# Attention with each score computed once, queries on partitions and weights turned by TensorE, in a one-core transformer layer

## The chip, the core and the metric

The kernel runs on one core of a Trainium2 chip. Its metric is the device time of one execution in microseconds (us): the median of three runs is 1499.16 us (1499.1 to 1499.41). The engines in the profile are TensorE (PE, with its weight loads as PEld), VectorE (DVE), ScalarE (ACT), GpSimd (POOL) and the sync engine (SP), which issues DMAs.

## The reference

One layer over 1024 positions of width 1024, all in float32. Two attentions run side by side, each with 8 heads of width 64, and a gated merge and a feed-forward block follow:

```python
h = rms_norm(x, norm1); proj = h @ w_in            # q,k,v of both attentions, forget logits, gates
# forgetting attention, causal:  c = cumsum(log_sigmoid(f))
sc = q @ k.T / 8 + c[query] - c[key];  p = softmax(where(key <= query, sc, -1e30));  o_a = p @ v
# band attention: own chunk of 64 and the 8 chunks before, plus a bias by clipped distance
sc = where(valid, q @ k.T / 8 + rel_bias[clip(query - key)], -1e30);  o_b = softmax(sc) @ v
merged = sigmoid(g_a) * (o_a @ w_branch_a) + sigmoid(g_b) * (o_b @ w_branch_b)
x = x + merged @ w_out
x = x + relu(rms_norm(x, norm2) @ w_up)**2 @ w_down;   return rms_norm(x, final_norm)
```

## The kernel before

Every product is made of matmuls on operands that are split in a high part (rounded to fp32r) and a low part (the rest). ACT makes the high part (L282 `split`, L167 for weights), DVE or POOL the low part (L283, L169), and TensorE adds high·high, high·low and low·high (`product`, L220). The stages follow one another: norm and first gates, the projections of q, k, v and the gates by Strassen units of 7 products (`strassen_steps`), attention, the branch products (`branch`, tiles `m`), the output product (`o`), the up projection and the down projection. q and k lie in DRAM for each head as `qk_dram` (128 rows: high parts twice against high and low) and `sk_dram` (64 rows: the remaining low part), v as `v_dram` (high and low halves).

Attention has 16 heads of 1024 queries, cut in 8 blocks of 128: first the 8 band heads (pairs `pr` 0 to 3, each query block sees up to 5 key blocks), then the 8 forgetting heads (`pr` 4 to 7, up to 8 key blocks). Each head takes two steps:

- `shifts` (two heads ahead of its use): scores with queries on partitions (L505, high parts only; L508 adds the causal mask by a matmul), a DVE instruction that adds the bias and takes the least value of a row (L512, sign turned, so this is the row's maximum), and a transpose of these 8 columns to a row in DRAM (L517, `m_rows`). It is needed for a safe softmax only.
- `attend`: scores again, now with keys on partitions (tiles `st`: L739 with `qk`, L747 with `sk`, whose extra rows carry masks and the row's shift; L755 adds the causal mask or the distance bias by more matmuls), ACT's exp (L759), a split of the weights `p` in `th` (ACT, L282) and `tl` (DVE, L283), and three matmuls into the output bank `pv` (L762, L763, L764). Columns of ones beside v give the row sums. ACT copies the bank out (L771, L774, L775), and `normalise` sends the row sums through DRAM, takes the reciprocal and multiplies (L793).

TensorE's and the other engines' order within attention is that of a scheduler, except where a call goes through `Ordered` (`TO`, `VO`, `AO`, `LO`), which keeps the program's order on that engine (its instructions all have one line, L96). `psg`, `pss`, `pst` and `psv` are PSUM pools of 1, 3, 3 and 1 banks. 16 fillers (`filler`, 12 matmuls each), the branch products of the heads that are done, run beside the forgetting heads. While the last two gate units (6 and 7) run, `shifts` of the first two heads are spread between their products by the table `AHEAD`. After the last head come the branch products of the forgetting heads (192 matmuls, L220 `m`, results joined by POOL at L846). Exp and sigmoid are different tables of ACT. The sigmoid of the gates is at L396, with the gates' stores to `z_dram`.

Of the kernel before, what the change touches and what calls it, by code (L numbers as in the profile page):

```python
# [18 lines left out]
P = 128  # L19
# [15 lines left out]
EARLY, AHEAD = 3, (0, 0, 0, 3, 4, 3, 3, 3)  # L35
LO_POOL = lambda n: False

BC, PB = 2, 5

SK = HD + 18  # L40

NORM = (2, 6, 10, 14)
BIAS = 1
GPOOL = ()
# [11 lines left out]
FILL = lambda n: 16 if n <= 18 else 16 - (n - 18) * 16 // 14  # L56

# [12 lines left out]
def pieces(width):  # L70
    if width <= 512:
        return [(0, max(width, 256), width)]
    if width - 512 >= 256:
        return [(0, 512, 512), (512, width - 512, width - 512)]
    return [(0, width - 256, width - 256), (width - 256, 256, 256)]
# [7 lines left out]
def hybrid_block(ctx: ExitStack, tc: tile.TileContext, xT, xN, g1, wall, wf, fb, relb, relt, rows, g2, g3, outT):  # L83
# [14 lines left out]
    VO, TO, AO, LO = Ordered(V), Ordered(T), Ordered(A), Ordered(nc.sync)  # L98
# [20 lines left out]
    identr = cpool.tile([P, P], F32R, tag="identr", name="identr")  # L119
    V.tensor_copy(identr, ident)  # L120

    masks = []
    for n, (step, cm) in enumerate(((-1, 1), (1, -1))):
        m = cpool.tile([P, 3, P], F32R, tag=f"mask{n}", name=f"mask{n}")
        raw = tmp("raw")[:, 0:3 * P].rearrange("p (n q) -> p n q", q=P)
        G.memset(raw, 0.0)
        G.affine_select(out=raw[:, 1, :], in_=raw[:, 1, :], compare_op=ALU.is_ge, fill=BIG, base=0,
                        pattern=[[step, P]], channel_multiplier=cm)
        G.tensor_copy(m, raw)
        masks.append(m)  # L130
# [8 lines left out]
    ncq = cpool.tile([P, 8, NH], F32, tag="ncq", name="ncq")  # L139
# [7 lines left out]
    m_rows = dram("m_rows", [16, 2, S])  # L147
    o_dram = dram("o_dram", [4, P, S])
    d_dram = dram("d_dram", [8, 2, S])
# [243 lines left out]
    def gate_out(ps, c, h, eng=V):  # L393
        t = etile("zt")
        eng.tensor_tensor(t, ps, rstd[:, hs(h)], op=ALU.mult)
        A.activation(t, t, AF.Sigmoid)  # L396
        store(z_dram[c, :, hs(h)], t)

# [49 lines left out]
    def forget_columns():  # L448
        pt = pst.tile([P, 8, NH], F32, tag="st", name="cqt")
        for h in range(2):  # L450
            c = tp.tile([NH, HALF], F32, tag="t", name="cr", bufs=8)
            load(c, c_dram[:, hs(h)])
            for i in range(4):
                T.transpose(pt[:, 4 * h + i, :], c[:, i * P:(i + 1) * P], ident[0:NH, 0:NH])
        V.tensor_scalar(ncq, pt, -1.0, None, op0=ALU.mult)

    heads = [(pr, hh) for pr in range(8) for hh in range(2)]

    def load_bias(pr, hh):

        fox = pr >= 4
        head = 2 * (pr % 4) + hh
        bc = aps.tile([P, S], F32, tag="bc", name=f"bc{pr}_{hh}", bufs=BC)
        if fox:
            load(bc, c_dram[head:head + 1, :].to_broadcast([P, S]))
            return bc, None, lambda: None
        load(bc[:, :BAND], relb[head])
        near = tmp("near")[:, 0:256]  # L470
        load(near, relt[head])
        far = aps.tile([P, 1], F32, tag="far", name="far", bufs=2)
        nb = [aps.tile([P, 256], F32R, tag="nb" + x, name=f"nb{x}{pr}_{hh}", bufs=3) for x in "hl"]

        def finish():
            tc.keep_in_program_order(V.tensor_copy(far, bc[:, 0:1]))
            for t in (bc[:, :BAND], near):
                A.activation(t, t, AF.Identity, scale=-1.0, bias=far)
            G.memset(bc[0:64, BAND - 64:BAND], BIG)
            G.memset(bc[64:128, 0:64], BIG)  # L480
            split(nb, near, G)

        return bc, nb, finish

    def load_head(pr, hh):
        qk = apq[(2 * pr + hh) % 3].tile([P, 2, S], F32R, tag="qk", name=f"qk{pr}_{hh}")
        loads.append(load_r(qk, qk_dram[2 * pr + hh]).ins)
        return qk

    loads = []  # L490

    def shifts(pr, hh, qk, bc, ps_s, ps_t):

        fox = pr >= 4
        mn = aps.tile([P, 8], F32, tag="mn", name=f"mn{pr}_{hh}", bufs=2)
        for i in range(8):
            j0 = 0 if fox else max(0, i - 4)
            W = (i + 1 - j0) * P
            st = aps.tile([P, 4], F32, tag="st", name="st", bufs=4)
            prev, x = 3.0e38, 0  # L500
            for s0, n, v in pieces(W):
                ks = j0 * P + s0
                ps = ps_s.tile([P, HALF], F32, tag="d", name="s")
                diag = fox and s0 + v == W
                T.matmul(ps[:, :n], qk[:, 1, i * P:(i + 1) * P], qk[:, 0, ks:ks + n], start=True, stop=not diag)  # L505
                if diag:
                    d = v - 256 if v > P else 0
                    T.matmul(ps[:, d:d + 256], identr, masks[0][:, 0:2, :] if v > P else masks[0][:, 1:3, :],  # L508
                             start=False, stop=True)
                b0 = s0 if fox else (4 - i + j0) * P + s0  # L510
                out = mn[:, i:i + 1] if s0 + v == W else st[:, x:x + 1]
                V.tensor_tensor_reduce(ps[:, :v], ps[:, :v], bc[:, b0:b0 + v], 1.0, prev, ALU.add, ALU.min, out)  # L512
                prev, x = out, x + 1
            if i < 7:
                yield
        pt = ps_t.tile([P, HALF], F32, tag="d", name="mt")
        T.transpose(pt[0:8, 0:P], mn, ident)  # L517
        mr = aps.tile([8, 2, P], F32R, tag="mr", name=f"mr{pr}_{hh}", bufs=2)
        split((mr[:, 0, :], mr[:, 1, :]), pt[0:8, 0:P], V)
        store(m_rows[2 * pr + hh].rearrange("r (i k) -> i r k", k=P), mr.bitcast(F32))  # L520
        yield
# [118 lines left out]
    tiles = [load_bias(*hd) for hd in heads[:2]]  # L640
    for t in tiles:
        t[2]()
# [10 lines left out]
    apq = [pool(astack, f"apq{n}", "right") for n in range(2)][::-1]  # L653
    for n in range(2):
        tiles[n] = (load_head(*heads[n]), *tiles[n])
    ahead = chain(*[shifts(*heads[n], *tiles[n][:2], psd[1], psd[1]) for n in range(2)])

    for n, ins in enumerate(chain(steps, last)):
        with tc.issue_after(ins):
            for _ in range(AHEAD[n]):  # L660
                next(ahead, None)
# [10 lines left out]
    ap_, apv, apq2, ap0 = [pool(astack, n, "right") for n in ("ap", "apv", "apq2", "ap0")]  # L672
    apq.append(apq2)
    psg = psum(astack, "psg", 1)
    pss = psum(astack, "pss", 3)
# [526 lines left out]
```

## Time and profile before

| | us |
|---|---|
| median of three runs | 1499.16 |
| span of the profiled execution, first to last instruction | 1494.2 |
| outside that span (median less span) | 5.0 |
| last gate product (start 418.2) to the first matmul of `attend` (430.3) | 12.1 |
| eight band heads, 430.3 to 560.6 | 130.3 |
| eight forgetting heads with 14 fillers, 560.6 to 722.2 | 161.6 |
| branch products and the last fillers, 722.2 to 771.7 | 49.5 |

A row of the timeline gives the start in us from the span's start, the length, the engine, the line, the tiles (written from read), the shape and the count. Matmul records overlap: each holds the time to its end in the array, so what a matmul takes of TensorE is read from one start to the next. A row of the groups ends with "busy us, mean ns of one | idle time of the engine before them and who ended it".

### The profile page before, as it was taken

The numbers are of one execution on the slowest core, as the hardware profiler recorded it, in microseconds if no ns is written. First come the engines' busy times: TensorE is split into PE (matmuls) and PEld (weight loads), VectorE is DVE, ScalarE is ACT, GpSimd is POOL, SyncE is SP. The second block draws the span as 40 slices with busy tenths as digits, with TensorE's granted clock in tenths as the row PEclk, the third lists the DMA queues.
The fourth block names the chain that finished last, engine by engine and source line by source line (L and its number), as shares of the span: only waits on it lengthen the run. The fifth ranks groups of instructions, "written<-read, shape, count | busy, mean of one in ns | idle before, by whom it ended". The sixth has DMA issues, their size and how long they took to land.

```text
span 1494.2 us, 21093 instructions
## 1 busy us (share of the span) xinstructions
PE 1451.0 (97%) x6810; PEld 1203.4 (81%) x6810; DVE 895.1 (60%) x1548; ACT 733.1 (49%) x1396; POOL 844.2 (57%) x715
## 2 busy tenths in 40 slices
PE   8999999999989999999999999999999999999996
PEld 5787888888878887788787878888888888888885
DVE  7755544533467878774425685555554557999644
ACT  8633333344358878666425453333333344444643
POOL 2467777777822332111095477777777645558463
PEclk9999999999989999999999999999999999999998
DMA  8546667764689698884566334444443876589263
GB/s 276 151 123 191 182 192 224 195 197 137 190 185 192 159 193 198 197 229 111 184 189 217 130 106 156 152 155 155 153 151 128 276 239 188 163 253 221 90 206 119
DMA packets 154126, 267.17 MB, mean 179 GB/s; under 512 B 22616, under 2 KB 42328, under 8 KB 150880
## 3 DMA queue, kind: packets, MB, share of 16 engines
q1 hardware_dynamic: 79632, 141.54, 31.3%
q10 hardware_dynamic: 50448, 83.75, 17.7%
q0 software_dynamic: 23936, 40.54, 12.6%
q8 instruction: 53, 0.87, 0.3%
q14 instruction: 57, 0.47, 0.1%
HBM read 179.42 MB, written 86.34 MB: 178 GB/s over the span
## 4 chain that ended last, share of the span: by engine, by line
PE 43%; POOL 3%; issue 2%; DMA 2%; DVE 1%; ACT 0%; SPq 0%; POOLq 0%; ACTq 0%; DVEq 0%
PE u L220 20%; PE dS L220 12%; PE dA L220 8%; PE o L220 4%; POOL ml L283 1%; POOL m L846 1%; DMA m<-m_dram 0%; DMA olt<-o_dram 0%; POOL wl_A L169 0%; DMA wr<-wall 0%; DMA rb<-r_dram 0%; DVE T2l L283 0%; DVE B22l L283 0%; POOL wl_o L169 0%; POOL accu L1037 0%
## 5 line engine op out<-in xcount | busy, mean ns | idle before, releaser
L169 POOL TENSOR_TENSOR wl_A<-wr,wh_A 128x512 fp32r<-128x512 f32 x118 | 156.6, 1335 | 89.1 <-ACT wh_A L167 71.1
L169 POOL TENSOR_TENSOR wl_S<-S,wh_S 128x512 fp32r<-128x512 f32 x102 | 135.5, 1332 | 34.0 <-ACT wh_S L167 32.7
L283 DVE TENSOR_TENSOR tl<-p,th 128x512 fp32r<-128x512 f32 (+1 forms) x192 | 107.8, 585 | 27.5 <-ACT th L282 26.4
L167 ACT CAST wh_S<-S 128x512 fp32r<-128x512 f32 x105 | 64.3, 621 | 121.0 <-PE u L220 65.5
L167 ACT CAST wh_A<-wr 128x512 fp32r<-128x512 f32 x105 | 65.1, 620 | 89.3 <-PE u L220 48.8
L169 POOL TENSOR_TENSOR wl_S<-ks,wh_S 128x512 fp32r<-128x512 f32 x48 | 68.8, 1460 | 51.9 <-ACT wh_S L96 48.6
L282 ACT CAST th<-p 128x512 fp32r<-128x512 f32 (+1 forms) x192 | 92.8, 510 | 9.6 <-PE pv L763 4.6
L578 DVE TENSOR_TENSOR u<-u,u 128x512 f32<-128x512 f32 x70 | 48.8, 697 | 67.9 <-PE u L220 67.9
L512 DVE CUSTOM_DVE_ANT_0 s<-s,bc 128x384 f32<-128x384 f32 (+3 forms) x128 | 69.8, 563 | 30.6 <-PE s L508 12.1
L190 POOL TENSOR_TENSOR S<-wr,wr 128x512 f32<-128x512 f32 x35 | 46.0, 1313 | 57.7 <-DMA wr<-wall 52.8
L505 PE MATMUL s<-qk 128*128 128x384 f32 (+2 forms) x192 | 64.2, 359 | 13.5 <-DMA qk<-qk_dram 9.0
L739 PE MATMUL st<-qk 128*128 128x512 f32 (+1 forms) x192 | 66.2, 348 | 0.6 <-ACT p L759 0.5
L762 PE MATMUL pv<-th,v 128*128 128x512 f32 (+1 forms) x192 | 65.9, 343 | 0.6 <-ACT on L775 0.6
L169 POOL TENSOR_TENSOR wl_A<-ka,wh_A 128x512 fp32r<-128x512 f32 x32 | 45.8, 1440 | 36.3 <-ACT wh_A L96 34.8
L747 PE MATMUL st<-sk 82*128 82x512 f32 (+1 forms) x192 | 65.6, 343 | 0.0
L759 ACT ACTIVATE p<-st,ncq 128x512 f32<-128x512 f32 (+1 forms) x96 | 54.5, 599 | 22.6 <-PE st L755 15.9
L763 PE MATMUL pv<-th,v 128*64 128x512 f32 (+1 forms) x192 | 65.3, 340 | 0.0
L764 PE MATMUL pv<-tl,v 128*128 128x512 f32 (+1 forms) x192 | 65.0, 339 | 0.0
L282 ACT CAST qkh<-qk 128x512 fp32r<-128x512 f32 x32 | 19.9, 621 | 89.5 <-DMA qk_dram<-qkl 43.3
L946 ACT ACTIVATE v<-v 128x512 f32<-128x512 f32 x64 | 40.3, 632 | 45.9 <-DVE v L945 45.9
L220 PE MATMUL u<-B22h,wh_S 128*128 128x512 f32 x140 | 54.8, 391 | 2.5 <-DVE c L569 2.5
L571 DVE TENSOR_TENSOR u<-u,c 128x512 f32<-128x512 f32 x35 | 24.5, 700 | 53.4 <-PE u L220 53.2
(399 smaller groups left out, 4905.4 us busy)
## 6 DMA issues: line engine op xcount, KB each, us to landing
wr<-wall SPq DMA_DIRECT2D x243, 256.0 KB
qk<-qk_dram POOLq DMA_DIRECT2D x16, 1024.0 KB, 6.1
a_dram<-at ACTq DMA_DIRECT2D x64, 256.0 KB
xT<-a_dram SPq DMA_DIRECT2D x64, 256.0 KB
qk_dram<-qkh ACTq DMA_DIRECT2D x96, 128.0 KB
a_dram<-v ACTq DMA_DIRECT2D x48, 256.0 KB
xB<-a_dram SPq DMA_DIRECT2D x44, 256.0 KB
z_dram<-zt ACTq DMA_DIRECT2D x32, 256.0 KB
```

The lines of the kernel that those rows point to most:

```text
L167: (act.tensor_copy if act is G else act.copy)(wh, src)
L169: lows.append(eng.tensor_tensor(wl, src, wh.bitcast(F32), op=ALU.subtract))
L220: done = eng.matmul(bank, w[wi], x[xi], start=(first and t == 0), stop=(t == n - 1 and not part), skip_group_check=part or not first)
L282: A.copy(dst[0], src)
L283: eng.tensor_tensor(dst[1], src, dst[0].bitcast(F32), op=ALU.subtract)
L505: T.matmul(ps[:, :n], qk[:, 1, i * P:(i + 1) * P], qk[:, 0, ks:ks + n], start=True, stop=not diag)
L512: V.tensor_tensor_reduce(ps[:, :v], ps[:, :v], bc[:, b0:b0 + v], 1.0, prev, ALU.add, ALU.min, out)
L739: T.matmul(ps[:, c], qk[:, 0, keys], qk[:, 1, qs], start=True, stop=False)
L747: T.matmul(ps[:, c], sk[:, 0, keys], sk[:, 1, qs], start=False, stop=not extra)
L762: T.matmul(pv[:, c], v3[hh][:, j, 1:3, :], th[:, c], start=first, stop=False)
L763: T.matmul(pv[0:HD, c], v3[hh][:, j, 0, :], th[:, c], start=False, stop=False)
L764: T.matmul(pv[:, c], v3[hh][:, j, 1:3, :], tl[:, c], start=False, stop=last)
```

## The change

Attention is written anew; the rest stays, apart from four small edits (below).

- The forgetting heads come first (`HEADS`). The fillers are now the branch products of the forgetting heads and run beside the last 7 of the 8 band heads (`FILL_FROM = 9`, each `F` in a string is 3 matmuls; 2 of 16 are left for the end). The band heads' outputs take the way over `o_dram`.
- `score` computes the scores of a query block once, queries on partitions, in a bank pair of 1024 columns (`pss`, 2 of them): 128-row `qk` and 64-row `sk`. The DVE instruction adds the bias and takes the row's least value in place (one instruction for band heads; for forgetting heads from the third block on two, of which the last takes 256 columns with the causal mask, which POOL adds in `make_bias`). `soften` is one exp over the whole row by ACT with the row's value as bias and the row sum as second result (`accum_out`). There are no mask and bias matmuls, no `m_rows`, no `ncq`, no columns of ones.
- `turn_p` turns the weights block by block by TensorE (`transpose`, float32, 36 blocks in a forgetting head and 30 in a band head, up to four into one bank); `turn` splits the bank in `th` (ACT) and `tl` (DVE, which now reads the bank and not SBUF). `weigh` is two matmuls for each run of blocks: v's high and low halves lie side by side in 128 columns, so that one pass gives both; ACT copies both halves of the bank out, and POOL adds them and multiplies with the reciprocals (`normalise`).
- TensorE's order in attention is written out: `S` (score and exp of one block), `T` (one bank of transposes and its split), `P` (the two passes of one bank), `F` (a quarter of a filler). Scores run 7 blocks ahead. Loads go through SP in program order (before: POOL's queue for `qk`, `sk` and `v`).
- Small edits: only 4 blocks of the first head are scored beside the gate units; exps wait for the last early sigmoid; the gates 14 and 15 get their sigmoid in the branch stage; one mask of 128 columns is made at the start in place of two of 384 and an fp32r identity.

```diff
-EARLY, AHEAD = 3, (0, 0, 0, 3, 4, 3, 3, 3)
+EARLY, AHEAD = 3, (0, 0, 0, 0, 1, 1, 2, 0)
+LATE_GATES = (14, 15)
+HEADS = [(pr, hh) for pr in (4, 5, 6, 7, 0, 1, 2, 3) for hh in range(2)]
+LEAD_S = 7
+FOX_TURN = "TSTTSPTSTPPSTTSPPTSTPSTPPSPP"
+BAND_TURN = "TFTSFFFSTPSTPTPSFTSFPTSPTFFPSPSP"
+FILL_FROM = 9
+def key_groups(pr, h):
+    if h == 0:
+        return [(0,), (1, 3), (2,)]
+    return [(0,), (1,), (2,), (3,), (4,), (5, 7), (6,)] if pr >= 4 else [(3,), (4,), (0, 2), (1, 6), (5, 7)]
...
+    def score(n, i, bank, te, ve):
...
+        for t, w in enumerate((qk, sk)):
+            for a, b in spans:
+                keys = slice(j0 * P + a - off, j0 * P + b - off)
+                te.matmul(bank[:, a:b], w[:, 1, rows], w[:, 0, keys], start=t == 0, stop=t == 1)
...
+        if pr < 4:
+            ve.tensor_tensor_reduce(x, x, bc[:, 0, b0:BAND], 1.0, 3.0e38, ALU.add, ALU.min, out)
+            return
...
+            ve.tensor_tensor_reduce(x, x, bc[:, 0, 0:W - 2 * P], 1.0, 3.0e38, ALU.add, ALU.min, prev)
...
+        ve.tensor_tensor_reduce(x, x, near, 1.0, prev, ALU.add, ALU.min, out)
+    def soften(n, i, bank):
...
+            A.activation(p[:, :W], bank[:, off:off + W], AF.Exp, scale=-1.0, bias=smalls[n][0][:, i:i + 1],
+                         accum_out=smalls["den", pr][:, 8 * hh + i:8 * hh + i + 1])
...
+    pss = psum(astack, "pss", 2)
+    pst = psum(astack, "pst", 2)
+    psv = psum(astack, "psv", 1)
+    psg = psum(astack, "psg", 1)
...
+    def turn_p(n, h, js):
...
+                TO.transpose(pt[:, x:x + P], probs[n, i][:, k:k + P], ident)
...
+    def weigh(n, h, js, first, last):
...
+            for t, src in enumerate((th, tl)):
+                TO.matmul(pv[:, b * P:(b + nb) * P], values[n][:, j, :], src[:, x:x + nb * P],
...
+            A.copy(outs[pr, h][rows], pv[HD:P])
+            A.copy(lows_o[pr, h][rows], pv[0:HD])
...
+    def turn():
...
+        A.copy(th, pt)
+        V.tensor_tensor(tl, pt, th.bitcast(F32), op=ALU.subtract)
```

On TensorE, in the middle of a forgetting head before: `st` are score banks with keys on partitions, `s` those for the maximum, `pv` the output bank, `identr` the identity by which masks are added.

```order
L505 MATMUL s_6337<-qk5_0_6165 128x256
L508 MATMUL s_6337<-mask0_75,identr_73 128x256
L505 MATMUL s_6355<-qk5_0_6165 128x512
L739 MATMUL st_6341<-qk4_0_5674 128x256
L747 MATMUL st_6341<-sk0_4176 128x256
L755 MATMUL st_6341<-mask1_82,identr_73 128x256
L762 MATMUL pv_6238<-th_6243,v30_4172 128x512
L763 MATMUL pv_6238<-th_6243,v30_4172 64x512
L764 MATMUL pv_6238<-tl_6244,v30_4172 128x512
```

The same engine in the middle of the third forgetting head (number 2) in the changed kernel: `s` is the score bank of the next head (3), `pt` the bank of turned weights, `p2_4` the weights of head 2 for query block 4, `ident` the float32 identity.

```order
L103 MATMUL s_4558<-qk3_4305 128x256
L103 MATMUL s_4558<-sk3_4306 128x256
L103 MATMUL pt_4564<-ident_66,p2_4_4436 128x128
L103 MATMUL pt_4564<-ident_66,p2_5_4456 128x128
L103 MATMUL pt_4564<-ident_66,p2_6_4476 128x128
L103 MATMUL pt_4564<-ident_66,p2_7_4512 128x128
L103 MATMUL pv_4546<-th_4523,v2_4285 128x384
L103 MATMUL pv_4546<-tl_4524,v2_4285 128x384
L103 MATMUL pv_4546<-th_4523,v2_4285 128x128
L103 MATMUL pv_4546<-tl_4524,v2_4285 128x128
```

Scores stand once and without masks, two `pv` passes stand for three, and the transposes are new; all of it now stands in program order.

On DVE, in a forgetting head before: `tl` reads the weights `p` from SBUF, and the row-minimum instruction (with the short instruction that reads its result) stands in two pieces for a wide block.

```order
L283 TENSOR_TENSOR tl_6256<-p_6254,th_6255 128x512
L512 ISA s_6334,st_6333<-s_6334,bc5_0_6167 128x512
L512 ISA st_6333 128x1
L283 TENSOR_TENSOR tl_6273<-p_6271,th_6272 128x512
L512 ISA s_6355,st_6354<-s_6355,bc5_0_6167 128x512
L512 ISA st_6354 128x1
L512 ISA s_6337,mn5_0_6209<-s_6337,bc5_0_6167,st_6333 128x256
L512 ISA mn5_0_6209 128x1
```

On DVE in the changed kernel, at the sixth block (number 5) of forgetting head 3, with the weights of head 2 turned between: `pt` is a PSUM bank.

```order
L847 TENSOR_TENSOR tl_4640<-pt_4638,th_4639 128x512
L505 ISA s_4649,st3_4540<-s_4649,bc3_4309 128x512
L505 ISA st3_4540 128x1
L847 TENSOR_TENSOR tl_4660<-pt_4658,th_4659 128x256
L511 ISA s_4649,mn3_4539<-s_4649,bc3_4309,st3_4540 128x256
L511 ISA mn3_4539 128x1
```

The kinds of instruction are the same; the low parts read PSUM, and each now waits for a transpose and a cast, and the exp of the next block waits for the second row-minimum instruction behind them.

More of the change, by code (lines that the diff above doesn't have):

```diff
@@ L446, in forget @@
         store(c_rows, e)
[L448 to L457, printed above, removed]
@@ L485, in load_head @@
[L485 to L521, printed above, removed]
@@ L639, in hybrid_block @@
     aps = pool(astack, "aps", "right")
-    tiles = [load_bias(*hd) for hd in heads[:2]]
-    for t in tiles:
-        t[2]()
+    for n in range(2):
+        load_bias(n, nc.sync)
+        make_bias(n)
     for g in range(EARLY_GATES // 2, 6):
```

426 lines of the change are left out of this document (231 added, 195 removed).

## The prediction

> **What bounds the kernel now.** First the page's head: TensorE is busy nearly throughout.
>
> ```profile
> span 1494.2 us, 21093 instructions
> PE 1451.0 (97%) x6810; PEld 1203.4 (81%) x6810; DVE 895.1 (60%) x1548; ACT 733.1 (49%) x1396; POOL 844.2 (57%) x715
> ```
>
> The change lies in one stage, so the next view is the busy time by stretches (columns: length, then each engine's busy time with its instructions, granted TensorE clock, DMA share, GB/s). I cut it at the last gate product, the first matmul of `attend`, the change from band to forgetting heads, the last `pv` matmul and the end of the branch products.
>
> ```profile
> 418.60:430.30 11.70, 6.18 (x26) 3.98 (x26) 7.38 (x30) 1.76 (x4) 1.82 (x2) 0.67 0.97 333
> 430.30:560.60 130.30, 124.38 (x755) 110.63 (x754) 99.89 (x312) 106.65 (x252) 37.21 (x60) 0.95 0.75 167
> 560.60:722.20 161.60, 156.87 (x835) 131.70 (x834) 110.20 (x273) 112.55 (x227) 27.78 (x34) 1.00 0.69 176
> 722.20:772.00 49.80, 48.47 (x211) 38.76 (x210) 14.85 (x22) 14.81 (x25) 26.59 (x22) 1.00 0.65 206
> ```
>
> In the two attention stretches TensorE is busy for 95 and 97%, but ACT for 82 and 70% and DVE for 77 and 68%: TensorE sets the pace, with little room on the others. A change that only relieves TensorE soon meets them.
>
> Third, what a matmul takes, from one start to the next in TensorE's timeline:
>
> ```profile
> 442.49 0.40 PE L763 MATMUL pv<-th,v 128*64 128x512 f32 x1
> 442.72 0.39 PE L764 MATMUL pv<-tl,v 128*128 128x512 f32 x1
> 442.95 0.33 PE L762 MATMUL pv<-th,v 128*128 128x384 f32 x1
> 443.12 0.34 PE L763 MATMUL pv<-th,v 128*64 128x384 f32 x1
> 443.29 0.28 PE L739 MATMUL st<-qk 128*128 128x256 f32 x1
> 443.41 0.28 PE L747 MATMUL st<-sk 82*128 82x256 f32 x1
> 443.53 0.22 PE L755 MATMUL st<-nbh,identr 128*128 128x128 f32 x1
> 443.59 0.27 PE L755 MATMUL st<-nbl,identr 128*128 128x128 f32 x1
> 443.70 0.39 PE L505 MATMUL s<-qk 128*128 128x384 f32 x1
> ...
> 101.53 1.03 PE L615 MATMUL vtp<-ident,vt 128*128 128x128 f32 x8
> 102.31 0.48 PE L220 MATMUL u<-B11h,wh_A 128*128 128x512 f32 x1
> ```
>
> 512 columns take 0.23 us, 384 take 0.17, 256 take 0.12, 128 take 0.06 or 0.11 (I use 0.09). Eight float32 transposes take 102.31 - 101.53 = 0.78, or 0.10 each.
>
> By these a forgetting head before costs TensorE: maxima 5x0.23 + 3x0.17 + 4x0.12 = 2.1, their masks 8x0.12 = 1.0; five passes (`qk`, `sk`, three `pv`) of 6x0.23 + 2x0.17 + 4x0.12 = 2.2, so 11.0; masks 1.0; with two fillers (24x0.23 = 5.5) 20.6, against 161.6/8 = 20.2 measured (the last two loops score no maxima). A band head: 1.8 + 5x1.92 + 18 bias matmuls at 0.11 = 13.4, against 130.3/8 = 16.3.
>
> **The change on TensorE.** Scores of a forgetting head are cut in pieces of 512 (6), 384 (2), 256 (2) and 128 (2): 2.14 a pass, two passes 4.3. 36 transposes: 3.6. The two value passes have the same pieces: 4.3. Together 12.2, where 15.1 stood. A band head: scores 1x512, 5x384, 5x256, 1x128 are 1.77, twice 3.5; 30 transposes 3.0; values 3x(0.23 + 0.17 + 0.12 + 0.09) = 1.83, twice 3.7; together 10.2. With 8 `F` (5.5) 15.7.
>
> The transposes are the one new kind of work, and here a page speaks against the change. The Trainium skill ("TensorE: Matmul & The Clock Gate", Part 4: PE-mode transpose) gives about 275 ns for a transpose in a kernel. By that figure, as an estimate, 36 would be 9.9 us and a head 18.5. The trace's record is 0.27 long too, but the starts are 0.10 apart, so the measurement decides.
>
> **ACT and DVE.** Their prices are in the groups (busy, mean ns of one, idle before):
>
> ```profile
> L759 ACT ACTIVATE p<-st,ncq 128x512 f32<-128x512 f32 x48 | 32.1, 689 | 10.6 <-PE st L747 4.8 <-PE st L755 4.1 <-DMA d_dram<-on 1.4
> L759 ACT ACTIVATE p<-st,ncq 128x256 f32<-128x256 f32 x32 | 14.8, 474 | 10.4 <-PE st L755 10.2
> L315 ACT ACTIVATION_READ_ACCUMULATOR rstd<-rstd 128x1 f32 x8 | 1.5, 187 | 0.0
> L282 ACT CAST th<-p 128x512 fp32r<-128x512 f32 x72 | 43.5, 619 | 2.1 <-DVE on L793 1.5
> L282 ACT CAST th<-p 128x256 fp32r<-128x256 f32 x80 | 31.4, 410 | 6.3 <-PE pv L763 3.7 <-DVE mn L512 1.0 <-DVE z L691 0.8
> L775 ACT COPY on<-pv 64x512 f32<-64x512 f32 x15 | 8.7, 578 | 0.4
> L512 DVE CUSTOM_DVE_ANT_0 s<-s,bc 128x512 f32<-128x512 f32 x38 | 26.6, 703 | 4.1 <-PE s L508 2.1 <-PE s L505 1.8
> L512 DVE CUSTOM_DVE_ANT_0 s<-s,bc 128x256 f32<-128x256 f32 x14 | 6.2, 443 | 0.1
> L512 DVE CUSTOM_DVE_ANT_0 s<-s,bc,st 128x256 f32<-128x256 f32 x40 | 19.3, 487 | 1.5 <-PE s L505 0.7 <-PE s L508 0.2
> L512 DVE DVE_READ_ACCUMULATOR2_ANT mn<- 128x1 f32 x112 | 15.9, 142 | 0.0
> L283 DVE TENSOR_TENSOR tl<-p,th 128x512 fp32r<-128x512 f32 x72 | 53.7, 757 | 16.0 <-ACT th L282 15.3 <-PE pv L764 0.5
> L691 DVE TENSOR_TENSOR z<-m,z 128x512 f32<-128x512 f32 x32 | 22.1, 691 | 49.8 <-DMA z<-z_dram 31.8 <-PE m L220 16.0 <-PE o L220 1.9
> L283 DVE TENSOR_TENSOR vs<-vtp,vs 128x256 fp32r<-128x256 f32 x32 | 12.7, 418 | 6.9 <-ACT vs L282 6.1 <-DMA qk_dram<-qkh 0.8
> ```
>
> An exp with a bias column costs 0.26 + 0.108 per 128 columns (the two `ncq` rows). A forgetting head has 8 exps over 36 blocks: 8x0.26 + 36x0.108 = 6.0, their sums 8x0.19 = 1.5, ten casts 8x0.62 + 2x0.41 = 5.8, four copies of the output bank 4x0.58 = 2.3: ACT 15.6. On DVE a row minimum costs 0.18 + 0.13 per 128 columns, 0.487 where it takes up an earlier piece, and 0.14 each to read: 14 of them are 0.31 + 0.44 + (6x0.18 + 21x0.13 = 3.8) + 6x0.49 + 14x0.14 = 9.5. The ten low parts now read PSUM, as the `z` and `vs` rows do: 8x0.69 + 2x0.42 = 6.4 (by the `tl` row, which reads SBUF alone, 0.5 more). DVE 15.9.
>
> So in a forgetting head DVE (15.9) and ACT (15.6) bound and TensorE's 12.2 is no longer the end. A band head: ACT 8x0.26 + 30x0.108 + 1.5 + 4.7 + 2.3 = 13.8, with filler weights 14.5; DVE 6.5 + 5.3 = 11.8, with filler results 13.4; TensorE 15.7 with fillers is the bound.
>
> **Coupling.** Each engine keeps its order, and there are two score banks: block i is scored when the exp of block i-2 is done. I walked one forgetting loop by hand along the order of PE, DVE and ACT with these prices and 0.1 to 0.2 us a hand-over. It repeats after 17.5 us: TensorE waits 1.3 us before the first block of the next head, 1.2 before its second (both for exps over 7 and 8 blocks), and some 2.5 more, mostly for exps and for the copies of the output bank. Band loops come to 16.3: the fillers fill those waits.
>
> The waits have a second price, the clock. These stretches lie on the grid of 3.41 us on which the clock changed:
>
> ```profile
> 484.05:487.46 3.41, 2.41 (x13) 1.51 (x11) 3.41 (x11) 3.34 (x9) 1.90 (x3) 1.00 0.03 5
> 487.46:490.87 3.41, 3.41 (x13) 2.71 (x12) 3.41 (x11) 1.69 (x5) 1.36 (x3) 0.50 0.28 49
> 490.87:494.28 3.41, 3.41 (x23) 3.18 (x22) 2.33 (x7) 2.54 (x6) 0.00 (x0) 1.00 1.12 365
> 617.17:620.58 3.41, 2.28 (x11) 1.14 (x9) 1.53 (x3) 3.41 (x10) 0.93 (x1) 1.00 1.10 288
> ```
>
> After a stretch with 2.41 us busy the next ran at half clock. After 2.28 busy with longer matmuls (617) the granted mean up to 722.2 stays 1.00. TensorE would be busy for 12.2/17.5 = 70%, 2.4 of 3.41: at that edge. A half-clock stretch costs at most 1.7 us, part of it absorbed by waits. I take 1.0 a forgetting loop: 18.5.
>
> **The sum, last gate product to last `pv`.** Start: 10, against 12.1. Then too the first matmuls need operands that load only as gate tiles come free. 1 MB of `qk` landed 6.1 us after issue (row below), and `sk` and the values follow, so about 8, and 2 for the low clock (0.67 before). Seven forgetting loops 7x18.5 = 129.5. The eighth scores band blocks: ACT 5.8 + 2.3 + 6.8 = 14.9 bounds, times 17.5/15.9 = 16.4. The first band loop has no fillers: 13.8x1.1 = 15.2. Six band loops 6x16.3 = 97.8. The last has hardly a score left: 12.8 on TensorE, say 13. Together 281.9, where 722.2 - 418.2 = 304.0 stood: -22.1. Fewer scores beside the gate units: -0.5.
>
> ```profile
> qk<-qk_dram POOLq DMA_DIRECT2D x16, 1024.0 KB, 6.1
> ```
>
> Rows for what I cost at nothing:
>
> ```profile
> L846 POOL TENSOR_TENSOR m<-m,z 128x512 f32<-128x512 f32 x16 | 20.9, 1308 | 14.8 <-DVE z L691 14.8
> L396 ACT ACTIVATE zt<-zt 128x512 f32<-128x512 f32 x32 | 19.7, 629 | 12.6 <-DVE zt L395 12.4
> L396 ACT ACT_TABLE_LOAD x2 | 2.6, 1283 | 0.0
> ```
>
> These are: the end (two fillers and 192 matmuls, about 49 us of TensorE, stand behind the last `pv` now as then; they hide the last normalisation, four POOL steps of 1.3 and two ways of a quarter megabyte over DRAM, each under the 6.1 of a whole one: under 18; without that cover so much more); the four late sigmoids of 0.63 (ACT has 14.8 busy in 49.8 there; uncovered 2.5 and 1.3 for each table); `make_bias` and `normalise` on POOL (28 busy in 161.6; DVE's PSUM reads keep 0.69 beside it); the masks at the start (off TensorE's way). Either way each is under 1 us if the cover holds.
>
> The profiled execution's span is 1494.2, the median of three runs 1499.16, so 5.0 lie outside it, kept as they are. 1499.2 - 22.6 = 1476.6, so **1477 us**. With bounds: forgetting loops at 15.9, band loops at their engines' sums and a start of 8 give 8 + 111 + 15 + 14 + 94 + 13 = 255, -49, 1450; loops 1.5 longer than taken (16 of them) give 1501.
>
> **Rivals.** (1) *Slower: the clock gate.* If transposes don't hold the clock, forgetting loops run at half clock: 2x12.2 = 24.4 us on TensorE, eight loops 8x24.4 = 195 in place of 146, +49: about 1526. It decides from a loop of 18.5 + 22.6/8 = 21.3 us: (21.3 - 17.5)/1.7 = 2.2 low stretches of its 6.2, a mean granted clock of 0.82. For it: the drop after 2.41 busy. Against: a half-clock TensorE is busy all the time, and that brought the clock back within one stretch at 490.87. The Trainium skill ("TensorE: Matmul & The Clock Gate", Part 4: PE-mode transpose) says that the full clock doesn't engage for transposes, since they don't count as busy in the same way; by that this rival would be the rule. The trace can't show it: the bursts at 101 are too short. (2) *No gain: coupling or SP's queue.* A head's loads (1 MB + 0.5 for `sk`, values and bias each) are 2.6 MB a loop, 150 GB/s of 17.5 us, in one queue behind waits for the end of a head; the stage moved 167 to 176 over several. Loops 1.4 longer by this or by tighter coupling, 16 times, give 1499. Against: the loads have a whole loop of lead. (3) *More gain*: the engines overlap to their bounds, 1450. Against: three engines within 30% of each other in strict order. That it doesn't do what it says, TensorE's work not falling, is excluded by the counts.
>
> **Chances.** The forecast (1460 to 1491) 0.60, more gain 0.13, no gain (1491 to 1505) 0.15, the clock 0.12. A difference of 0.2% (3 us) is about what a measurement of this kernel can tell from none. Faster: 0.60 + 0.13 + 0.07 = 0.80; same 0.07; slower 0.13. The range 1455 to 1501 leaves out half of (3) and the clock.
>
> **What would show it.** Right: attention 22 us shorter; forgetting loops near 18 with DVE and ACT over 85% busy and TensorE near 70%; transposes 0.10 apart; band loops near 16 with TensorE busy. Wrong: a granted clock under 0.82 in the forgetting stage; idle of `s` ended by loads; loops over 20; a gap in the branch stage.

## The result and the profile after

The changed kernel takes 1488.88 us (median of 7 runs, 1486.83 to 1492.46) against 1499.16 (7 runs, 1492.36 to 1503.78): a ratio of 0.9937, 95% interval 0.9918 to 0.9957. It is faster by 0.63%, some 10 us, where 22 were forecast.

The page's head shows that TensorE is still busy for 97% of the span, although the attention has lost its second score.

```profile
span 1490.5 us, 20539 instructions
PE 1449.7 (97%) x6666; PEld 1168.3 (78%) x6666; DVE 863.4 (58%) x1424; ACT 721.9 (48%) x1389; POOL 872.1 (59%) x697
```

This execution took 1492.2 us, 1.7 more than its span, so the 5.0 us that the prediction put outside the span were mostly something else. If before has the same 1.7 outside its span, its profiled execution took 1495.9 us (1494.2 + 1.7) and was one of the quicker ones. That is why the two spans differ by 3.7 us and the medians by 10.3.

The next view is the busy time by stretches (length, busy time of PE, PEld, DVE, ACT and POOL with their instructions, granted clock, DMA share, GB/s). I cut it from the last gate product at the end of each head, which is the copy of its low half (`lo`, L791): the start with the first loop, the six forgetting loops behind it, the loop that turns the last forgetting head and scores band blocks, the first band loop (no fillers), the six with fillers, the last head, the branch products.

```profile
419.81:447.50 27.69, 25.57 (x104) 17.67 (x102) 18.42 (x52) 15.06 (x33) 2.53 (x2) 0.75 0.33 96
447.50:552.80 105.30, 97.92 (x509) 69.14 (x507) 78.71 (x231) 80.89 (x184) 41.12 (x37) 0.98 0.60 164
552.80:570.70 17.90, 15.87 (x90) 11.50 (x88) 11.66 (x29) 13.66 (x33) 3.39 (x4) 1.00 0.59 166
570.70:588.90 18.20, 16.46 (x78) 12.46 (x77) 10.23 (x24) 12.49 (x29) 10.76 (x11) 0.81 0.57 162
588.90:704.70 115.80, 115.74 (x617) 88.21 (x616) 70.48 (x159) 75.58 (x177) 33.43 (x33) 1.00 0.68 208
704.70:720.60 15.90, 14.35 (x84) 11.74 (x83) 7.35 (x13) 11.10 (x22) 6.87 (x6) 1.00 0.48 150
720.60:769.95 49.35, 48.53 (x213) 39.41 (x211) 14.48 (x20) 15.71 (x27) 34.51 (x28) 1.00 0.70 234
```

Against the forecast: start and first loop 27.7 (28.5), six forgetting loops 105.3 or 17.55 each (111), the eighth 17.9 (16.4), the first band loop 18.2 (15.2), six band loops 115.8 or 19.3 each (97.8), the last 15.9 (13). The excess is 18.9 us in all. The six band loops with fillers, where TensorE is busy for 115.74 of 115.80 us, have 18.0 too much; the three other band and mixed loops are 7.4 over, and the start and the forgetting loops are 6.5 under.

What a matmul takes there is read from one start to the next. This piece of TensorE's timeline is from the second of these loops.

```profile
613.32 0.28 PE L103 MATMUL s<-qk 128*128 128x256 f32 x1
613.53 0.38 PE L103 MATMUL s<-sk 64*128 64x256 f32 x1
613.84 0.66 PE L103 MATMUL pt<-ident,p 128*128 128x128 f32 x4
...
614.86 0.62 PE L103 MATMUL pt<-ident,p 128*128 128x128 f32 x4
615.24 0.36 PE L103 MATMUL pv<-th,v 128*128 128x256 f32 x1
615.44 0.28 PE L103 MATMUL pv<-tl,v 128*128 128x256 f32 x1
615.56 0.33 PE L103 MATMUL s<-qk 128*128 128x384 f32 x1
615.82 0.43 PE L103 MATMUL s<-sk 64*128 64x384 f32 x1
616.18 0.50 PE L103 MATMUL m<-oh,wh_ab 128*128 128x512 f32 x1
616.52 0.39 PE L103 MATMUL m<-ol,wh_ab 128*128 128x512 f32 x1
```

The `pv` pass of 256 columns takes 0.12 us where the next matmul has weights of 128 rows too (615.44 to 615.56), as before. But the score of 256 columns takes 0.21 ahead of the 64-row `sk`, and `sk` itself 0.31 ahead of the next 128-row weights; with 384 columns it is 0.26 and 0.36 instead of 0.17. In these rows each change between 128 and 64 rows costs 0.1 to 0.2 us. Smaller surcharges stand behind the change (the first filler matmul takes 0.34, from 616.18 to 616.52, for 0.23) and behind a group of transposes (the first `pv` pass 0.20 for 0.12). The weight loads of the same loop say how (engine PEld, in brackets the time for which the loader stood and what ended it):

```profile
609.00 0.30 PEld L103 LDWEIGHTS s<-qk 128*128 128x128 f32 x2
609.50 0.29 PEld L103 LDWEIGHTS s<-sk 64*128 64x128 f32 x2 [0.19 <-issue]
609.98 0.19 PEld L103 LDWEIGHTS m<-oh,wh_ab 128*128 128x128 f32 x1 [0.19 <-issue]
610.09 0.19 PEld L103 LDWEIGHTS m<-ol,wh_ab 128*128 128x128 f32 x1
```

The loads of `qk` to `qk` and of `oh` to `ol` run ahead, beside the matmul in front of them. The two at a change of rows stand for 0.19 us each, waiting for nothing that the profile shows.

Summed from the starts of all matmuls in the six filled loops, a loop takes 19.3 us of TensorE: scores 6.0 (`qk` 2.7, `sk` 3.3), transposes 2.8, values 4.3, fillers 6.1. The forecast had 3.5, 3.0, 3.7 and 5.5.

### The profile page after: what moved, and what is told of

Read it like the earlier page. It is cut to its first block, busy times and chain, and to the rows that moved or that the text cites. A ratio compares the mean times of both kernels' runs of the same rounds, so it can differ in the third digit from the quotient of the medians.

```text
span 1490.5 us, 20539 instructions
## 1 busy us (share of the span) xinstructions
PE 1449.7 (97%) x6666; PEld 1168.3 (78%) x6666; DVE 863.4 (58%) x1424; ACT 721.9 (48%) x1389; POOL 872.1 (59%) x697
## 3 DMA queue, kind: packets, MB, share of 16 engines
q10 hardware_dynamic: 44368, 77.19, 16.4%
## 4 chain that ended last, share of the span: by engine, by line
PE 81%; ACT 4%; POOL 4%; issue 4%; DMA 3%; DVE 3%; ACTq 1%; SPq 0%; POOLq 0%; DVEq 0%
PE u L215 41%; PE dS L215 12%; PE s L103 5%; PE dA L215 5%; PE pv L103 4%; PE pt L103 4%; PE o L215 4%; PE m L103 3%; PE m L215 1%; POOL wl_A L164 1%; POOL m L899 1%; DMA xT<-a_dram 1%; POOL ml L278 1%; ACT p L522 1%; DMA bc<-relb 1%
## 5 line engine op out<-in xcount | busy, mean ns | idle before, releaser
L522 ACT ACTIVATE p<-s,mn 128x640 f32<-128x640 f32 (+7 forms) x128 | 89.9, 703 | 46.8 <-DVE mn L511 21.6
L847 DVE TENSOR_TENSOR tl<-pt,th 128x512 fp32r<-128x512 f32 (+1 forms) x144 | 90.9, 643 | 16.7 <-ACT th L846 16.3
L103 PE MATMUL pt<-ident,p 128*128 128x128 f32 x528 | 87.4, 289 | 7.9 <-ACT p L522 4.9
L846 ACT CAST th<-pt 128x512 fp32r<-128x512 f32 (+1 forms) x144 | 76.4, 550 | 38.0 <-PE pt L103 36.8
L103 PEld LDWEIGHTS pt<-ident,p 128*128 128x128 f32 x528 | 61.7, 145 | 29.8 <-issue 10.8
L809 POOL TENSOR_TENSOR on<-on,lo 128x512 f32<-128x512 f32 x16 | 20.5, 1280 | 96.6 <-ACT lo L791 96.6
L500 DVE CUSTOM_DVE_ANT_0 s<-s,bc 128x640 f32<-128x640 f32 (+2 forms) x64 | 42.6, 666 | 50.5 <-PE s L103 45.8
L103 PE MATMUL s<-sk 64*128 64x256 f32 (+2 forms) x188 | 65.0, 400 | 0.0
L103 PE MATMUL s<-qk 128*128 128x256 f32 (+2 forms) x188 | 57.7, 362 | 5.4 <-ACT p L522 4.7
L164 POOL TENSOR_TENSOR wl_S<-wr,wh_S 128x512 fp32r<-128x512 f32 x34 | 45.1, 1328 | 24.0 <-ACT wh_S L162 23.9
```

What stands on the lines that cost most here:

```text
L103: return lambda *a, **kw: tc.keep_in_program_order(getattr(self.eng, name)(*a, **kw))
L164: lows.append(eng.tensor_tensor(wl, src, wh.bitcast(F32), op=ALU.subtract))
L500: ve.tensor_tensor_reduce(x, x, bc[:, 0, b0:BAND], 1.0, 3.0e38, ALU.add, ALU.min, out)
L522: A.activation(p[:, :W], bank[:, off:off + W], AF.Exp, scale=-1.0, bias=smalls[n][0][:, i:i + 1], accum_out=smalls["den", pr][:, 8 * hh + ...
L809: G.tensor_tensor(o, o, lows_o[pr, h], op=ALU.add)
L846: A.copy(th, pt)
```

## The experiments

**The theories.** A: the row counts. `sk` has 64 rows and stands between weights of 128 rows; each of its 8 scores a head pays for two changes. In before `sk` had 82 rows, and the row that priced it showed no such cost. B: the float32 transposes break the loads ahead and hold TensorE up. C, told in the first expectation: score matmuls are slow because ACT and DVE use PSUM at the same time. The rival to all: a chain of waits through two score banks sets the loops, whatever TensorE's work costs. Each ratio is to the kernel before on the same chip.

### `sk` in 128 rows

```diff
-        sk = p.tile([HD, 2, S], F32R, tag="sk", name=f"sk{n}")
+        if n < 2:
+            sks.append(p.tile([P, 2, S], F32R, tag="sk", name=f"sk{n}"))
+            G.memset(sks[n][HD:P].bitcast(F32), 0.0)
+        sk = sks[n % 2]
...
-        loads.append(eng.dma_start(sk.bitcast(F32), sk_dram[e]).ins)
+        loads.append(eng.dma_start(sk[0:HD].bitcast(F32), sk_dram[e]).ins)
```

> sk, the 64-row operand of the scores, lies in 128 rows of which 64 are zero; nothing else is changed. Theory A (a matmul on 64-row weights can't have its weights loaded ahead of a matmul on 128 rows, nor the other way round, so each change between the two costs TensorE about 0.2 us, 16 times a head): band loops with fillers fall from 19.3 to about 16.3 us, the two passes of a score take equally long, and the whole gains about 20 us over the changed kernel, near 1468. Theory B (the float32 transposes are what costs: 0.109 us each, and 0.09 more for the matmul behind a group): no change, loops stay at 19.3. Theory C (score matmuls are slow because ACT and DVE use PSUM at the same time): no change.

Measured: 1465.0 us (1453.57 to 1467.03), ratio 0.9732 (0.967 to 0.9794). That is 24 us less than the change as it was by the medians, 28 by the profiled spans (1490.5 and 1462.3) and 31 by the two ratios; the two kernels were measured beside different runs of before. The same products now follow each other without the gap (TensorE's timeline of this kernel):

```profile
601.25 0.46 PE L103 MATMUL s<-qk 128*128 128x384 f32 x2
601.54 0.46 PE L103 MATMUL s<-sk 128*128 128x384 f32 x2
601.83 0.28 PE L103 MATMUL pv<-th,v 128*128 128x256 f32 x1
```

384 and 256 columns together take 0.29 us a pass for `qk` and for `sk`, as 0.17 + 0.12 in before. The stretches, six forgetting loops, the first band loop and the six filled ones:

```profile
439.80:536.40 96.60, 86.47 (x509) 71.30 (x509) 78.65 (x231) 80.22 (x185) 41.29 (x37) 0.96 0.68 179
553.60:569.80 16.20, 13.39 (x80) 11.74 (x79) 10.28 (x24) 12.21 (x30) 10.28 (x9) 0.89 0.66 182
569.80:675.50 105.70, 100.38 (x617) 87.92 (x616) 69.27 (x159) 75.38 (x178) 33.87 (x36) 1.00 0.76 228
```

That is 16.1, 16.2 and 17.6 us a loop. The scores of a filled loop fell from 6.0 to 3.9 us of TensorE by their starts, everything else stayed within 0.3, and 0.9 us of idle time came in. From the last gate product to the last `pv` it is 273.2 us where the changed kernel had 299.5. A is confirmed, and C falls. 18.8 of the 26.3 us lie in these twelve loops. 4.9 lie in the start with the first loop (27.7 to 22.8), where the granted clock was 0.93 and not 0.75 as before the edit, so there rows and clock aren't parted. The last head, which has hardly a score, took 17.0 us and not 15.9.

The loads show it too. These are the groups of the loader in the six filled loops, first the changed kernel, then the one with 128 rows:

```profile
L103 PEld LDWEIGHTS s<-sk 64*128 64x128 f32 x72 | 11.5, 184 | 9.7 <-issue 9.7
L103 PEld LDWEIGHTS s<-sk 128*128 128x128 f32 x72 | 11.9, 189 | 0.5
```

A load takes as long with 64 rows as with 128 (184 and 189 ns); what goes is the standing before it, 9.7 us.

### `sk` in 66 rows

The same edit with 66 in place of `P`: two rows of zeros.

> sk lies in 66 rows of which 2 are zero. Theory A in its sharp form (only operands of up to 64 rows are held in a part of the array): as with 128 rows, band loops about 16.3 us, near 1468. In a loose form (any row count that differs from 128 costs the change): no gain, loops at 19.3. Theories B and C: no change.

Measured: 1465.37 us (1457.68 to 1466.09), ratio 0.9739 (0.9683 to 0.9794), not to be told from 128 rows. The groups of this kernel's filled loops (569 to 676 us) beside those of the changed kernel, first the changed kernel:

```profile
L103 PE MATMUL s<-sk 64*128 64x384 f32 x30 | 13.2, 438 | 0.0
L103 PE MATMUL s<-sk 64*128 64x256 f32 x30 | 8.9, 297 | 0.0
```

And with 66 rows:

```profile
L103 PE MATMUL s<-sk 66*128 66x384 f32 x30 | 10.4, 346 | 0.0
L103 PE MATMUL s<-sk 66*128 66x256 f32 x31 | 8.9, 286 | 0.0
```

A record holds more than what a matmul takes of TensorE, so the starts decide (timeline with 66 rows):

```profile
600.87 0.46 PE L103 MATMUL s<-qk 128*128 128x384 f32 x2
601.17 0.46 PE L103 MATMUL s<-sk 66*128 66x384 f32 x2
601.46 0.29 PE L103 MATMUL pv<-th,v 128*128 128x256 f32 x1
```

384 and 256 columns take 0.30 and 0.29 us, as with 128 rows; by all starts of six filled loops the scores take 4.0 us a loop (3.9 with 128 rows, 6.0 with 64). So it isn't the share of rows that are used: 66 rows show no surcharge, 64 do. 65 wasn't tried.

### Turned by fp32r matmuls

```diff
+    identr = cpool.tile([P, P], F32R, tag="identr", name="identr")
+    V.tensor_copy(identr, ident)
...
-        p = probs[n, i] = app.tile([P, (i + 1) * P], F32, tag=f"p{i}", name=f"p{n}_{i}")
+        p = probs[n, i] = app.tile([P, (i + 1) * P], F32R, tag=f"p{i}", name=f"p{n}_{i}")
...
-                TO.transpose(pt[:, x:x + P], probs[n, i][:, k:k + P], ident)
+                TO.matmul(pt[:, x:x + P], probs[n, i][:, k:k + P], identr, start=True, stop=True)
```

> The weights are written as fp32r by the exp and turned by ordinary fp32r matmuls with an fp32r identity, in place of float32 transposes; this leaves out the low part of the weights. sk keeps its 64 rows. Theory B: the turned blocks cost 0.06 to 0.09 in place of 0.109 and the matmul behind a group no extra 0.09, so 30 blocks and 8 groups save 1.2 to 2.2 us of a filled band loop and more if the transposes hold the array up otherwise: loops at 17 or less. Theory A: the changes of row count stay, at most 1.2 to 2.2 are saved, loops at 17.1 to 18.1, and the forgetting loops stay at 17 to 17.5, since DVE bounds them: a gain of 7 to 13 us over the changed kernel.

Measured: 1575.56 us (1563.5 to 1581.88), ratio 1.0474 (1.0403 to 1.0545). The gain that B asks for didn't come: within a group the turns still start 0.110 us apart (0.109 before the edit; medians in the filled loops). What came was not expected by any theory. The stretches are nine loops, of which eight have no fillers, and the last five with fillers:

```profile
450.50:689.70 239.20, 231.85 (x775) 172.16 (x774) 116.82 (x311) 121.81 (x273) 61.09 (x58) 0.59 0.40 115
689.70:787.40 97.70, 97.66 (x514) 75.56 (x513) 58.67 (x132) 63.25 (x149) 27.52 (x27) 1.00 0.65 202
```

The granted clock is 0.59 for 239 us, although TensorE is busy for 97% of them. It isn't low all the time: it comes back five times, for 7 to 10 us each, and falls again. The longest low piece and one of the five:

```profile
583.80:682.70 98.90, 97.23 (x294) 73.33 (x295) 40.20 (x100) 45.55 (x104) 20.50 (x22) 0.50 0.36 104
474.60:481.30 6.70, 5.57 (x31) 4.05 (x29) 4.60 (x13) 5.05 (x11) 3.84 (x4) 1.00 0.62 225
```

The first filled loop still ran in it; the five behind, at full clock, take 19.5 us each, no less than with transposes (19.3). So B falls. And rival (1) of the prediction, the clock gate, is a state that a kernel with the same loops and another kind of turn does fall into.

### No fillers beside the heads

```diff
-FILL_FROM = 9
+FILL_FROM = 99
...
     for _ in fills:
-        pass
+        flush(1)
     flush()
```

> No filler runs beside the heads; all 16 follow after the last one (14 more than before, 39 us of TensorE). If TensorE bounds the filled band loops (theories A and B), the loops fall by most of the 6 us that fillers take, to 14.5 to 16, and the whole gets slower by only 39 - 7 x 4 = 10 to 15 us. If the loops are bound by the chain of waits between engines (a rival), they stay at 18 or more, as the unfilled loop at 570.7 did, and the whole gets slower by 30 us.

Measured: 1535.32 us (1530.59 to 1541.49), ratio 1.022 (1.0149 to 1.029), 46 us over the changed kernel by the medians and 42 by the ratios, and so more than either theory asked for. The seven band loops:

```profile
567.30:689.90 122.60, 108.81 (x553) 82.34 (x550) 73.17 (x171) 83.72 (x200) 34.99 (x37) 0.89 0.55 151
```

They take 17.5 us each without 8 `F`, against 19.3 with them: fillers of 6.1 us cost 1.8. The loops don't fall to 13.2 us, which is what is left of TensorE's 19.3 without them. By the starts TensorE's work fills 15.5 of the 17.5 us and 2.0 are idle, mostly until DVE's `tl` is done. The work is longer than 13.2 at a granted clock of 0.89, where it was 1.00 with fillers. So 17.5 lies between the two forecasts: waits make 2.0 of the missing 4.3 us, the rest goes with the clock, and no run parts the two further. TensorE's own matmuls are 82% of the chain that ended last in these loops, so it isn't a chain apart from TensorE's work, as the rival has it. The part of the slowdown that neither had is in the tail, where the fillers now stand alone (a group of the stretch from 705 to 800):

```profile
L103 PE MATMUL m<-oh,wh_ab 128*128 128x512 f32 x64 | 27.4, 429 | 15.5 <-DVE z L742 11.6 <-POOL on L810 3.9
```

TensorE stands for 11.6 us there until DVE has read the fillers' one bank, and 3.9 for the last normalisation.

### Zero low parts, with transposes and with matmuls

These two part two readings of the low clock: that fp32r turns count less as work for the gate than float32 transposes (G1), or that the low parts, which are zero once the weights are rounded, make the second `pv` pass count less (G2). First float32 transposes of rounded weights, then the fp32r turns with a second operand that isn't zero (the sum in place of the difference).

```diff
-        p = probs[n, i] = app.tile([P, (i + 1) * P], F32, tag=f"p{i}", name=f"p{n}_{i}")
+        p = probs[n, i] = app.tile([P, (i + 1) * P], F32R, tag=f"p{i}", name=f"p{n}_{i}")
...
-                TO.transpose(pt[:, x:x + P], probs[n, i][:, k:k + P], ident)
+                TO.transpose(pt[:, x:x + P], probs[n, i][:, k:k + P].bitcast(F32), ident)
```

> As the changed kernel (64-row sk, float32 transposes), but the exp writes the weights rounded to fp32r, so that their low parts, and every moving value of the second value pass, are zero; this leaves out the low part of the weights. It separates two reasons for the low clock of the run with fp32r turns (granted mean 0.59 in the unfilled loops). Theory G1 (ordinary fp32r matmuls of 128 columns count less for the clock gate than float32 transposes): the clock stays as in the changed kernel, unfilled loops at 17 to 18, near 1489. Theory G2 (zeros in the low pass count as no work): the clock is low here too, unfilled loops near 26, near 1575.

The second is the edit of the fp32r turns and

```diff
-        V.tensor_tensor(tl, pt, th.bitcast(F32), op=ALU.subtract)
+        V.tensor_tensor(tl, pt, th.bitcast(F32), op=ALU.add)
```

> As the run with fp32r turns, but the second operand is the sum of the turned weights and their high part in place of the difference, so that nothing is zero; the values are wrong by this and the low part is left out. Theory G1: the clock is as low as there, unfilled loops near 26, near 1575. Theory G2: the clock is that of the changed kernel, unfilled loops at 17 to 18, filled ones at 19.5 as there, near 1489.

Measured: 1489.61 us, ratio 0.9935 (0.9901 to 0.9968), and 1573.38, ratio 1.0486 (1.0448 to 1.0524). The six forgetting loops with transposes and zeros:

```profile
447.00:552.40 105.40, 98.05 (x509) 69.12 (x507) 78.67 (x231) 80.91 (x185) 41.10 (x37) 0.98 0.56 164
```

The loops without fillers of the fp32r turns with a second operand that isn't zero:

```profile
453.20:662.30 209.10, 201.76 (x671) 149.05 (x669) 105.11 (x284) 108.74 (x244) 55.29 (x52) 0.58 0.40 111
```

The clock follows the kind of turn (0.98 and 0.58) and not the values. G2 falls and G1 agrees with both runs. The edit changes the number format and the transpose instruction together; which of the two it is wasn't tried.

### 128 rows and filler operands fetched earlier

With 128 rows, filler matmuls waited for their weights (groups of that kernel's six filled loops):

```profile
L103 PE MATMUL m<-oh,wh_ab 128*128 128x512 f32 x48 | 19.9, 414 | 2.0 <-ACT wh_ab L727 2.0
L103 PE MATMUL m<-oh,wl_ab 128*128 128x512 f32 x49 | 19.5, 399 | 1.4 <-POOL wl_ab L729 1.4
```

Three units are now fetched ahead, not one.

```diff
-        fetch()
+        for _ in range(3):
+            fetch()
...
-            if n + 1 < len(todo):
+            if n + 3 < len(todo):
                 fetch()
```

> sk in 128 rows as before, and the fillers' weights and gates are fetched three units ahead in place of one. In the run with 128 rows TensorE sat idle 3.4 us in six filled loops for weights of fillers. If these waits are on the path, the filled loops fall from 17.6 to about 17 and the whole gains 3 to 4 us more, near 1461; if other waits take their place, it stays within 2 us of 1465.

Measured: 1461.22 us (1458.74 to 1465.03), ratio 0.9739 (0.9704 to 0.9774). The fillers' idle is gone, but the loops aren't shorter (105.6 us for six, as 105.7): the idle now stands mostly before the scores, 3.2 us for ACT's `p`, and before the transposes, 1.8 for DVE's `tl` (1.4 already before this edit; the groups of its filled loops). In all it is 5.0 us for six loops, where it was 5.3.

```profile
L103 PE MATMUL pt<-ident,p 128*128 128x128 f32 x176 | 27.8, 278 | 1.8 <-DVE tl L852 1.8
...
L103 PE MATMUL m<-oh,wh_ab 128*128 128x512 f32 x47 | 19.9, 423 | 0.0
L103 PE MATMUL s<-qk 128*128 128x384 f32 (+1 forms) x70 | 19.5, 331 | 3.2 <-ACT p L526 3.2
```

Against 128 rows alone (0.9732) it can't be told apart. Both beat the two kernels of this study.

### The kernel before with 64 rows

If A is right, before must lose when its second score matmul uses 64 of the 82 rows. The rows past 64, which carry masks and row shifts, are left out, so the exp gets a scale that keeps it finite; the control has that exp alone.

```diff
-                T.matmul(ps[:, c], sk[:, 0, keys], sk[:, 1, qs], start=False, stop=not extra)
+                T.matmul(ps[:, c], sk[0:HD, 0, keys], sk[0:HD, 1, qs], start=False, stop=not extra)
...
-                A.activation(p[:, c], ps[:, c], AF.Exp, scale=-1.0, bias=ncq[:, j, head:head + 1] if fox else 0.0)
+                A.activation(p[:, c], ps[:, c], AF.Exp, scale=-1e-6, bias=epsb if fox else 0.0)
```

> The kernel before, with the second score matmul of each chunk cut from 82 rows to the 64 of sk alone; this leaves out the masks and shifts that the other 18 rows carry, and the exp gets a scale of a millionth and a constant bias so that nothing overflows. Theory A (each change between 128-row and 64-row weights costs TensorE about 0.2 us): 192 chunks with two changes each are 77 us more on the engine that bounds this kernel, so 60 to 77 us slower than before. A rival (the loss belongs to the changed kernel's written order or to its transposes): no change, within 5 us of before.

> The control for the run with 64 rows: the kernel before with the same exp (scale of a millionth, constant bias; the weights are wrong by this) and all 82 rows. All theories: as before, within 5 us; if not, the difference of the two runs is what 64 rows cost.

Measured: 1557.61 us (1556.73 to 1561.44), ratio 1.0375 (1.0343 to 1.0407), and for the control 1502.75 (1496.04 to 1508.57), ratio 1.0001 (0.9976 to 1.0027). TensorE's timeline with 64 rows, where the prediction's rows had 0.12 us for each of the same two steps:

```profile
450.76 0.28 PE L739 MATMUL st<-qk 128*128 128x256 f32 x1
450.98 0.38 PE L747 MATMUL st<-sk 64*128 64x256 f32 x1
451.29 0.39 PE L505 MATMUL s<-qk 128*128 128x256 f32 x1
```

They take 0.22 and 0.31. Fewer rows of the same matmuls cost 55 us by the control and 58 by before on the same chip (1499.91), 0.14 to 0.15 for each of the 384 changes between row counts. The forecast of 60 to 77 was a little high. So the row count has this price without the transposes, the new fillers or the new order.

## Why the prediction was wrong

The time lies within the stated range and even within 1460 to 1491, since both are wide; the gain is 10 us of the 22.6 that were forecast, and the terms show where it went.

**The step that failed** is "scores 1x512, 5x384, 5x256, 1x128 are 1.77, twice 3.5 ... With 8 `F` (5.5) 15.7". A filled band loop has 19.3 us of TensorE. 2.5 of the 3.6 us are in the scores (6.0 for 3.5), because `sk` was priced by the prediction's own row `st<-sk 82*128`, a form that the changed kernel doesn't have: it drops the rows of masks and shifts, and with them falls to 64. The diff shows it (`sk` is a tile of `HD` rows), and no row that the prediction used stood for it. With the rows padded, the scores measure 3.9. So the mechanism was right here (one score less on TensorE, transposes more, filled band loops bound by TensorE), and this term was mis-sized. That the padded kernel comes to 1465.0, 12 us under the forecast, isn't this term's doing: its forgetting loops take 16.1 us, for which the prediction had 18.5. The prediction's own sum of a band head before, 13.4 for 16.3 measured, had shown that a sum of such rows can come out too low (a forgetting head came to 20.6 for 20.2); it went on without asking why.

**The other terms.** Values measure 4.3 for 3.7 and the fillers 6.1 for 5.5, with surcharges behind transposes and behind `sk` that the sums didn't have; with the rows padded they are 4.1 and 5.8. The transposes, 2.8 for 3.0, were about right. By TensorE's starts the scores make 15 of the 18 us that six filled loops are over. Padding gave back 10.1 of them (115.8 to 105.7 us): TensorE's work fell from 19.3 to 16.7 us a loop, and 0.9 of idle came in its place.

**Forgetting loops.** 17.55 us, and the walk by hand had 17.5, but not for its reasons; that was luck. DVE 15.9 and ACT 15.6 are right as sums of durations, yet the busy time is 78.71 and 80.89 of 105.30, 75 and 77% and not "over 85%": records on one engine overlap at their ends, and on DVE the read of a row's result lies beside the next instruction. In DVE's timeline the row minimum ends at 471.23, and both the read and the next low part start at 471.15:

```profile
470.80 0.43 DVE L511 CUSTOM_DVE_ANT_1 s<-s,bc 128x256 f32<-128x256 f32 x1 [1.06 <-ACT p L522]
471.15 0.14 DVE L511 DVE_READ_ACCUMULATOR2_ANT mn<- 128x1 f32 x1
471.15 1.51 DVE L847 TENSOR_TENSOR tl<-pt,th 128x512 fp32r<-128x512 f32 x2
```

TensorE has 16.3 us a loop by its starts, not 12.2 (scores 7.0 for 4.3, transposes 4.1 for 3.6, values 5.2 for 4.3), and 1.2 of idle; with 128 rows 14.4 and 1.7. So it came near the bound again, and "TensorE near 70%" was wrong: 97.92 of 105.30, and TensorE's matmuls are 79% of the chain that ended last in these loops. DVE and ACT as the bound of the forgetting loops is the second step that failed.

**Loops without fillers, and the end of attention.** 18.2 for 15.2, 17.9 for 16.4, 15.9 for 13: all were summed from one engine. In the first two TensorE's starts fill 16.0 us (at a granted clock of 0.81) and 15.7, and the rest is idle time. In the last, which has fillers but hardly a score, they fill 14.3 for the 12.8 forecast.

**Rival (1), the clock.** It didn't come in this kernel as a steady state: the granted clock is 0.98 in the six forgetting loops, for which the prediction took 1 us each. It is low in the band loop without fillers (0.81) and in the start with the first forgetting loop (0.75), where it is half for 13.6 us:

```profile
423.40:437.00 13.60, 12.74 (x39) 8.86 (x39) 7.19 (x21) 7.15 (x17) 0.00 (x0) 0.50 0.56 152
```

The argument against the rival, that a half-clock TensorE is busy all the time and so gets its clock back, doesn't hold in general: with fp32r turns it stayed at 0.50 for 98.9 us with 98% busy, though it did come back in other places. The Trainium skill ("TensorE: Matmul & The Clock Gate", Part 4: PE-mode transpose) says that the full clock doesn't engage for transposes; here the traces say the reverse, 0.98 with float32 transposes against 0.59 with matmuls in their place.

**Rival (2), no gain.** SP's queue cost nothing: no idle of `s` in the six forgetting loops is ended by a load. Coupling shows as TensorE's idle time, 1.2 us of a forgetting loop and 1.7 to 2.0 of a loop without fillers, and none in the filled loops of the changed kernel.

**At nothing.** The cover at the end held: 49.35 us of branch products, 49.8 before. The start and first loop are 27.7 for 28.5; their low clock wasn't foreseen at this length, so that the sum comes out is luck in part.

**Open.** Why the clock stays up with float32 transposes and not with fp32r matmuls of the same size and distance; the values are excluded, number format and instruction aren't parted. What sets a filled loop with 128 rows at 17.6 us, of which TensorE's starts fill 16.7: the idle moved when the fillers' operands came earlier, and no single wait was shown to hold it. Whether fetching earlier is worth its 4 us.

## What to carry to other kernels

Price a matmul by a row of the same form, row count included. A contraction of 64 rows between contractions of 128 cost 0.1 to 0.2 us at each change here, and two rows of zeros took that away. Test such a sum on the kernel before, and follow up what it misses. Count only part of an engine's relief as time: here 2.6 us less work of TensorE in a filled loop were 1.7 us of time, and 1.9 less in a forgetting loop 1.45, because idle time came in.

## What the runs showed of the hardware

- In these runs weight loads ran ahead of the matmul in front where both have over 64 rows (66, 82 and 128 were tried), and didn't at a change between 64 and 128 (0.19 us of standing in the loader). Among 64-row weights alone it wasn't tried. The Trainium skill ("TensorE: Matmul & The Clock Gate", Part 2: Step-by-step: what each phase is for) has the time of a load go by its columns and says that the row count doesn't matter. The trace agrees for the load itself, 184 ns with 64 rows and 189 with 128. The price of 64 rows lies in when the load can start, and not in its length.
- A busy TensorE can stay at half clock: 98.9 us at 0.50 while 98% busy, within 239 us at 0.59, with turns by fp32r matmuls of 128 columns. Nine loops took 26.6 us each, near the 24.4 by which the prediction priced its rival (1); but that figure was twice the mis-sized 12.2, so the nearness is chance.
- Reading a row's result after a DVE instruction (0.14 us) took no time of its own where a low part followed (both start at 471.15). For ACT's read (0.19 us) this isn't shown.
